# First pair's in, out and query projections as three products of float32r parts, in a transformer-like trunk on one Trainium2 core

## Chip, cores, metric

One core of one Trainium2 chip runs the whole program. The metric is the time of one execution on the device, in microseconds (us), as the median of several runs. The engines named below: TensorE (PE in the rows; its weight loads PEld), VectorE (DVE), ScalarE (ACT), GpSimd (POOL) and SyncE (SP), which issues most transfers.

## What is computed

One layer on 1024 tokens of width 1024: a normalised input goes through an in-projection to three token mixers (a gated depthwise convolution of width 31, a short gated convolution of width 3, a gated block mixing), then through an out-projection; a query projection and product keys choose 16 of 16384 single-neuron experts for each of 8 heads; the chosen experts' rows are applied; an input embedding gate and a final norm end it.

```python
a = rmsnorm(h, g_mix[i])
z = a @ w_in[i]
za, zb, zc = z[..., :768], z[..., 768:1536], z[..., 1536:]
...
h = h + jnp.concatenate([ya, yb, yc], axis=-1) @ w_out[i]
...
q = (nf @ w_q).reshape(t, PEER_HEADS, D_KEY)
s1 = jnp.einsum("thd,hkd->thk", q1, sub_keys[:, 0])
v1, i1 = lax.top_k(s1, TOPK)
...
act = jax.nn.gelu(jnp.einsum("td,tkd->tk", xb, expert_u[ib])) * gb
out = jnp.einsum("tk,tkd->td", act, expert_v[ib])
```

## The kernel before

The 1024 tokens are eight tiles of 128 (the partition width). The front works on pairs of tiles, (0,1), (2,3), (4,5), (6,7); T = 256 columns a pair. `mix_in` (L139) loads and normalises the pair's rows, transposes them into `aT` (L148, 8 chunks of 128 inputs x 256 tokens) and makes 15 chunks of 128 outputs in `zchunks` (L152: one 512 KB weight tile `w1` and 8 float32 matmuls a chunk, into the PSUM tile `z`), and three more with `aT` as the stationary side (L201 to L208, the tile `vn`). The convolution (L177 to L180) is 30 x 3 VectorE steps `cacc = ya * ch + cacc`, all three tiles in SBUF. Statistics of `vn` follow (L209 to L223; the power of -1/2, `rv`, L220, is GpSimd's), then a mixing product (L232), a group norm of the convolution (L239 to L252), and the 8 chunks of `yT`.

`mix_out` (L255) multiplies `yT` with `w_out` (L267, 256 float32 records a pair), adds the residual (L269), normalises and transposes into `nT`. `choose` (L283) makes the queries, 16 chunks of 8 matmuls (L299), the key scores (L306), 16 best of each by VectorE (`top16`, L327) and `select` (L335), whose last step writes the gather index `idx` (L392).

Four of the tiles (`DENSE`, 1 to 4) go through all experts in a later stage, three (`GATHER`, 5 to 7) gather rows, and the `MIXED` tile 0 does its first half by gathers in the front: `u_step` (L524) issues 128 row gathers on GpSimd's queue (L536) with a VectorE dot product each (L538), and `gate_table` (L394) builds tables with VectorE, GpSimd (`oh2`, L421), ScalarE and TensorE. The dense stage starts when these are done, after some 1090 us; there and at the end of the program the products are already made of float32r parts: `hi` by a ScalarE cast, `lo = full - hi` by a GpSimd subtraction (L468 and L470), and three products hi*hi, hi*lo, lo*hi (L481 to L483).

A framework's scheduler sets the order on each engine when the program is built, from the program's order and its own estimates; each engine then runs its list strictly in that order and waits on semaphores. Small pools hold what rotates: `gathF` has three tiles `g` and one `hrow` for the gathers; `wstream` two each of `w1`, `wo`, `w3` for weights; `wbp` two tiles `st` for the tables.

## Time and profile before

| | us |
|---|---|
| median of 3 runs (2859.8 to 2860.92) | 2860.1 |
| the profiled execution | 2848.63 |
| its span, first to last instruction | 2846.6 |
| TensorE busy | 2607.7 (92%) |
| VectorE busy | 2163.0 (76%) |
| GpSimd busy | 1951.6 (69%) |
| ScalarE busy | 1007.2 (35%) |

The busy share is an average over stages with different limits; the dense stage, from some 1090 us on, holds most of TensorE's time. The change lies in the first 350 us, so the rows further down are read by stretch. Matmuls are pipelined: a single record's length says less than the time of a run of them divided by their number. A float32 matmul stands in the trace as two records.

### The profile page before, as it was taken

To read this page: it belongs to the slowest core of one execution; us is meant where nothing else is said; L and a number is where in the kernel's file an instruction comes from. 1 tells how busy PE (TensorE), PEld (TensorE's weight loads), DVE (VectorE), ACT (ScalarE), POOL (GpSimd) and SP (SyncE) were. 2 spreads that over 40 slices of the span, in tenths; PEclk is the share of its full clock that TensorE was granted. 3 is DMA by queue.
4 is the path that set the end of the run, shared out by engine and by line. 5 is a ranking of instruction groups with operands and counts; after the bars stand their busy time and mean duration, and the time that the engine had idled before them with its cause. 6 is when DMAs were issued, how large, how long until landed. Compare 5 with 4: busy or idle time off the path is not lost.

```text
span 2846.6 us, 37627 instructions
## 1 busy us (share of the span) xinstructions
PE 2607.7 (92%) x12671; PEld 2197.8 (77%) x12671; DVE 2163.0 (76%) x4738; ACT 1007.2 (35%) x1930; POOL 1951.6 (69%) x1740
## 2 busy tenths in 40 slices
PE   7999989798768568999999999999999999999988
PEld 6888878787767556888787888878788787888777
DVE  5566998899977886777777777776777777777776
ACT  3324237345655534232322223222232322222352
POOL 0000067368776787887888878887887878888783
PEclk9999999899778779999999999999999999999999
DMA  6354577787757559999999999999999999999885
GB/s 209 121 194 146 190 269 275 283 299 268 236 210 268 207 211 337 329 338 334 330 346 326 336 343 344 337 332 335 335 335 325 332 351 323 341 337 328 312 290 174
DMA packets 299697, 820.92 MB, mean 288 GB/s; under 512 B 26096, under 2 KB 117616, under 8 KB 296944
## 3 DMA queue, kind: packets, MB, share of 16 engines
q0 software_dynamic: 129024, 469.82, 45.9%
q1 hardware_dynamic: 170480, 348.70, 36.0%
q8 instruction: 100, 1.64, 0.2%
q14 instruction: 93, 0.76, 0.1%
HBM read 764.93 MB, written 53.48 MB: 288 GB/s over the span
## 4 chain that ended last, share of the span: by engine, by line
PE 43%; DVE 18%; DMA 18%; POOL 11%; issue 8%; ACT 1%; SPq 0%; POOLq 0%; DVEq 0%; ACTq 0%
DMA g<-expert_u,idx 8%; DMA g<-expert_v,idx 7%; PE mm L504 5%; PE mm L505 5%; PE mm L506 5%; PE z L481 5%; PE z L482 5%; PE z L483 5%; DVE g L538 4%; POOL g L536 3%; PE z L158 3%; PE mm L612 3%; POOL oh L421 3%; POOL vl L477 3%; PE mm L299 2%
## 5 line engine op out<-in xcount | busy, mean ns | idle before, releaser
L536 POOL DMA_INDIRECT g<-expert_u,idx x512 | 509.5, 995 | 340.1 <-DVE g L538 137.1
L568 DVE SCALAR_TENSOR_TENSOR accP<-g,act,accP 128x1024 f32<-128x1024 f32 x384 | 493.6, 1285 | 205.3 <-DMA g<-expert_v,idx 199.9
L538 DVE SCALAR_TENSOR_TENSOR g<-g,nP 128x1024 f32<-128x1024 f32 x352 | 423.2, 1215 | 168.9 <-DMA g<-expert_u,idx 167.7
L566 POOL DMA_INDIRECT g<-expert_v,idx x384 | 367.2, 956 | 143.4 <-DVE accP L568 62.0
L504 PE MATMUL mm<-vh,ah 128*128 128x512 f32 x1024 | 399.8, 392 | 16.1 <-DVE accA L508 8.8
L481 PE MATMUL z<-nh,uh 128*128 128x512 f32 x1024 | 401.5, 392 | 8.1 <-DVE al L490 5.9
L482 PE MATMUL z<-nl,uh 128*128 128x512 f32 x1024 | 400.2, 391 | 1.6 <-DVE nl L446 1.5
L483 PE MATMUL z<-nh,ul 128*128 128x512 f32 x1024 | 399.8, 390 | 0.0
L505 PE MATMUL mm<-vl,ah 128*128 128x512 f32 x1024 | 398.7, 390 | 0.0
L506 PE MATMUL mm<-vh,al 128*128 128x512 f32 x1024 | 396.4, 390 | 0.0
L421 POOL TENSOR_SCALAR oh<-iota,eT,gT 128x128 f32<-128x128 f32 x320 | 325.2, 1024 | 43.7 <-PE gt L430 39.0
L430 PE MATMUL gt<-oh,oh 128*128 128x128 f32 x1280 | 228.0, 327 | 131.6 <-DVE oh L415 69.7
L468 ACT CAST uh<-u 128x1024 fp32r<-128x1024 f32 x128 | 134.7, 1052 | 566.9 <-PE z L482 449.5
L477 POOL TENSOR_TENSOR vl<-v,vh 128x512 fp32r<-128x512 f32 x256 | 327.5, 1300 | 2.6
L430 PEld LDWEIGHTS gt<-oh,oh 128*128 128x128 f32 x1280 | 199.5, 229 | 160.7 <-POOL oh L421 92.1
L470 POOL TENSOR_TENSOR ul<-u,uh 128x1024 fp32r<-128x1024 f32 x128 | 308.7, 2412 | 3.9 <-ACT uh L468 1.9
L475 ACT CAST vh<-v 128x512 fp32r<-128x512 f32 x256 | 153.7, 621 | 319.1 <-DMA v<-expert_v 266.6
L538 DVE SCALAR_TENSOR_TENSOR g<-g,hrow 128x1024 f32<-128x1024 f32 x160 | 196.4, 1230 | 74.5 <-DMA g<-expert_u,idx 74.3
L299 PE MATMUL mm<-nT,w 128*128 128x256 f32 x1024 | 243.1, 387 | 0.0
L504 PEld LDWEIGHTS mm<-vh,ah 128*128 128x128 f32 x1024 | 193.0, 189 | 59.3 <-DVE accA L508 11.8
L508 DVE TENSOR_TENSOR accA<-mm,accA 128x512 f32<-128x512 f32 x320 | 218.1, 685 | 26.2 <-PE mm L506 25.6
L481 PEld LDWEIGHTS z<-nh,uh 128*128 128x128 f32 x1024 | 193.6, 189 | 53.0 <-DVE al L490 10.6
(367 smaller groups left out, 4593.6 us busy)
## 6 DMA issues: line engine op xcount, KB each, us to landing
u<-expert_uT SPq DMA_DIRECT2D x128, 512.0 KB, 6.1
v<-expert_v SPq DMA_DIRECT2D x128, 512.0 KB, 5.0
Wd<-st SPq DMA_DIRECT2D x20, 2048.0 KB, 8.9
w<-w_q SPq DMA_DIRECT2D x64, 512.0 KB, 4.5
w<-Wd SPq DMA_DIRECT2D x128, 256.0 KB, 10.2
w<-w_inF SPq DMA_DIRECT2D x60, 512.0 KB, 4.1
wo<-w_out SPq DMA_DIRECT2D x32, 512.0 KB, 3.4
g<-expert_u,idx POOLq DMA_INDIRECT x512, 6.2
```

Of the source, the lines that this page charges most:

```text
L421: nc.gpsimd.tensor_scalar(oh2[:, k], iota, k2, gk, op0=OP.is_equal, op1=OP.mult)
L430: nc.tensor.matmul(pw[:, :, k], oh2[:, k], oh1[:, k], start=True, stop=True)
L477: nc.gpsimd.tensor_tensor(vl, v[:, s * 512:s * 512 + 512], vh.bitcast(F32), op=OP.subtract)
L481: nc.tensor.matmul(ph, uh[:, c], nh[:, c], start=c == 0, stop=False)
L482: nc.tensor.matmul(ph, uh[:, c], nl[:, c], start=False, stop=False)
L483: nc.tensor.matmul(ph, ul[:, c], nh[:, c], start=False, stop=c == 7)
L504: nc.tensor.matmul(po, ah[:, c], vh, start=i == 0, stop=False)
L505: nc.tensor.matmul(po, ah[:, c], vl, start=False, stop=False)
L506: nc.tensor.matmul(po, al[:, c], vh, start=False, stop=i == NG - 1)
L536: nc.gpsimd.indirect_dma_start(out=ug, out_offset=None, in_=expert_u, in_offset=bass.IndirectOffsetOnAxis(ap=idx[:, k:k + 1], axis=0))
L538: nc.vector.scalar_tensor_tensor(ug, ug, 1.0, ns[t, front], op0=OP.mult, op1=OP.mult, accum_out=dots[:, k - b * KB:k - b * KB + 1])
L568: nc.vector.scalar_tensor_tensor(acc, vg, act[:, k:k + 1], acc, op0=OP.mult, op1=OP.add)
```

## The change

For the first pair (`t0` = 0) alone, the three projections are computed from float32r parts. `in_halves` splits the activations into `hi` (ScalarE) and `lo` (GpSimd), 16 pieces of 128x128 each for `aT` and `nT`, 8 of 128x256 for `yT`; they lie in the three `g` tiles and `hrow` of the gather pool. `weight_halves` splits one or two weight chunks of 128x1024 into a tile `st` of the pool that the gate tables use later. `add_up` adds 24 products for each output in place of 8. Two weight chunks are taken at a time; the raw weights alternate between two pairs of buffers. The three narrow chunks of the in-projection are computed 256 columns wide (the odd one with a repeated operand), and the out-projection two chunks of 128 columns at a time.

```diff
@@ -74,6 +74,10 @@
     nTd = dram.tile([P, 8, NA * P], F32, name="nTd")
     TG = 32
     Wd = {t: dram.tile([P, P // TG, P, TG], F32, name=f"Wd{t}") for t in TABLE}
+
+
+    SPLIT_IN, SPLIT_OUT, SPLIT_Q = (0,), (0,), (0,)
+    CHUNKS = (3, 4, 5, 6, 7, 0, 1, 2)
 
     fctx = ExitStack()
     work = fctx.enter_context(tc.tile_pool(name="work", bufs=2))
@@ -134,7 +138,34 @@
                 for c in range(4):
                     nc.scalar.activation(dst[:, c0 + c], pt[:, c], AF.Copy, scale=g[:, c0 + c:c0 + c + 1])
 
-    picks, keys, weights = {}, {}, {}
+    def in_halves(full, parts, order=range(8)):
+
+        T = full.shape[2]
+        lie = [gath.tile([P, 4, T], F32R, name=n, bufs=b) for n, b in (("g", FG), ("g", FG), ("g", FG), ("hrow", 1))]
+        hi = {c: lie[2 * (i // 4)][:, i % 4] for i, c in enumerate(order)}
+        lo = {c: lie[2 * (i // 4) + 1][:, i % 4] for i, c in enumerate(order)}
+        for p in parts:
+            for c in order:
+                nc.scalar.copy(hi[c][:, p], full[:, c, p])
+                nc.gpsimd.tensor_tensor(lo[c][:, p], full[:, c, p], hi[c][:, p].bitcast(F32), op=OP.subtract)
+        return [(hi[c], lo[c]) for c in range(8)]
+
+    def weight_halves(*raws):
+
+        w = wbp.tile([P, 2, 2, 8, P], F32R, name="st")
+        for i, raw in enumerate(raws):
+            nc.scalar.copy(w[:, 0, i], raw)
+            nc.gpsimd.tensor_tensor(w[:, 1, i], raw, w[:, 0, i].bitcast(F32), op=OP.subtract)
+        return w
+
+    def add_up(out, a, b):
+
+        order = CHUNKS
+        steps = [(a[c][x_], b[c][y_]) for x_, y_ in ((0, 0), (0, 1), (1, 0)) for c in order]
+        for i, (a_, b_) in enumerate(steps):
+            nc.tensor.matmul(out, a_, b_, start=i == 0, stop=i == len(steps) - 1)
+
+    picks, keys, weights, turn = {}, {}, {}, [0]
 
     def mix_in(t0, nt):
 
@@ -147,10 +178,22 @@
             nc.scalar.activation(a, a, AF.Copy, scale=r)
             transpose_rows(aT[:, :, t * P:(t + 1) * P], a, g_mix, tag="z")
 
+        if t0 in SPLIT_IN:
+            aH = in_halves(aT, [slice(t * P, (t + 1) * P) for t in range(nt)])
         yT = group.tile([P, 8, T], F32, name="yT")
 
         def zchunks(*js):
             pz = psum.tile([P, 2, T], F32, name="z")
+            if t0 in SPLIT_IN:
+                raws = []
+                turn[0] += 1
+                for j in js:
+                    raws.append(wstream.tile([P, 8, P], F32, name=("w1", "w3")[turn[0] % 2], bufs=2))
+                    nc.sync.dma_start(raws[-1], w_inF[j])
+                w = weight_halves(*raws)
+                for i in range(len(js)):
+                    add_up(pz[:, i], [(w[:, 0, i, c], w[:, 1, i, c]) for c in range(8)], aH)
+                return [pz[:, i] for i in range(len(js))]
             for i, j in enumerate(js):
                 w = wstream.tile([P, 8, P], F32, name="w1", bufs=2)
                 nc.sync.dma_start(w, w_inF[j])
@@ -198,7 +241,21 @@
 
 
         vn = group.tile([P, nt, 384], F32, name="vn")
-        for s in range(3):
+        for ss in ((0, 1), (2,)) if t0 in SPLIT_IN else ():
+            raws = []
+            turn[0] += 1
+            for s in ss:
+                raws.append(wstream.tile([P, 8, P], F32, name=("w1", "w3")[turn[0] % 2], bufs=2))
+                nc.sync.dma_start(raws[-1], w_inV[s])
+            w, n = weight_halves(*raws), len(ss)
+
+            wh, wl = [w[:, x_] if n == 2 else w[:, x_, 0:1].to_broadcast([P, 2, 8, P]) for x_ in range(2)]
+            for t in range(nt):
+                pv = psum.tile([P, 2, P], F32, name="z")
+                p = slice(t * P, (t + 1) * P)
+                add_up(pv, [(h_[:, p], l_[:, p]) for h_, l_ in aH], [(wh[:, :, c], wl[:, :, c]) for c in range(8)])
+                nc.scalar.copy(vn[:, t, ss[0] * P:(ss[0] + n) * P].rearrange("p (a c) -> p a c", a=n), pv[:, 0:n])
+        for s in () if t0 in SPLIT_IN else range(3):
             wv = wstream.tile([P, 8, P], F32, name="w1", bufs=2)
             nc.sync.dma_start(wv, w_inV[s])
             for t in range(nt):
@@ -258,7 +315,23 @@
         nT = group.tile([P, 8, T], F32, name="nT")
         hs = rowp.tile([P, nt, D], F32, name="h", bufs=1)
         nc.sync.dma_start(hs, x[t0 * P:(t0 + nt) * P].rearrange("(t p) d -> p t d", p=P))
-        for s in range(8):
+        if t0 in SPLIT_OUT:
+            yH = in_halves(yT, [slice(0, T)], CHUNKS)
+        for s in range(0, 8, 2) if t0 in SPLIT_OUT else ():
+            raws = []
+            for i in range(2):
+                raws.append(wstream.tile([P, 8, P], F32, name=("wo", "w3")[s // 2 % 2], bufs=2))
+                nc.sync.dma_start(raws[-1], w_out[s + i])
+            w = weight_halves(*raws)
+            po = psum.tile([P, nt, 2 * P], F32, name="mm")
+            for t in range(nt):
+                p = slice(t * P, (t + 1) * P)
+                add_up(po[:, t].rearrange("p (a c) -> p a c", a=2), [(h_[:, p], l_[:, p]) for h_, l_ in yH],
+                       [(w[:, 0, :, c], w[:, 1, :, c]) for c in range(8)])
+            h = hs[:, :, s * P:s * P + 2 * P]
+            nc.vector.tensor_add(h, po, h)
+            fill()
+        for s in () if t0 in SPLIT_OUT else range(8):
             w = wstream.tile([P, 8, P], F32, name="wo", bufs=2)
             nc.sync.dma_start(w, w_out[s])
             po = psum.tile([P, nt, P], F32, name="mm")
@@ -278,6 +351,8 @@
         if own:
             a0 = DENSE.index(t0 + own[0]) * P
             nc.sync.dma_start(nTd[:, :, a0:a0 + len(own) * P], nT[:, :, own[0] * P:(own[-1] + 1) * P])
+        if t0 in SPLIT_Q:
+            return in_halves(nT, [slice(t * P, (t + 1) * P) for t in range(nt)])
         return nT
 
     def choose(t0, nt, nT):
@@ -292,7 +367,15 @@
             pq = psum.tile([P, 2, T], F32, name="mm")
             sk = wstream.tile([P, 2, P], F32, name="sk", bufs=2)
             nc.sync.dma_start(sk, skT[:, 2 * h:2 * h + 2])
-            for side in range(2):
+            if t0 in SPLIT_Q:
+                raws = []
+                for side in range(2):
+                    raws.append(wstream.tile([P, 8, P], F32, name=("w3", "wo")[h % 2], bufs=2))
+                    nc.sync.dma_start(raws[-1], w_q[2 * h + side])
+                w = weight_halves(*raws)
+                for side in range(2):
+                    add_up(pq[:, side], [(w[:, 0, side, c], w[:, 1, side, c]) for c in range(8)], nT)
+            for side in () if t0 in SPLIT_Q else range(2):
                 w = wstream.tile([P, 8, P], F32, name="w3", bufs=2)
                 nc.sync.dma_start(w, w_q[2 * h + side])
                 for c in range(8):

```

Three places show how the order on the engines moves. First GpSimd, from its first `r` on (before: the norm factors `r`, `rB` and `rv`, and nothing else up to the gathers):

```order
L122 TENSOR_TENSOR r_150<-ss_147,half 128x1
L122 TENSOR_TENSOR r_177<-ss_174,half 128x1
L122 TENSOR_TENSOR r_862<-ss_859,half 128x1
L122 TENSOR_TENSOR r_889<-ss_886,half 128x1
L220 TENSOR_TENSOR rv<-st,half 128x6 x2
L122 TENSOR_TENSOR r_2748<-ss_2745,half 128x1
L122 TENSOR_TENSOR r_2775<-ss_2772,half 128x1
L122 TENSOR_TENSOR rB<-ss_818,half 128x1
L122 TENSOR_TENSOR rB<-ss_837,half 128x1
L220 TENSOR_TENSOR rv<-st,half 128x6 x2
```

and now (`st<-w` is the low part of a weight chunk, `g` and `hrow` low parts of `aT`):

```order
L126 TENSOR_TENSOR r_150<-ss_147,half 128x1
L126 TENSOR_TENSOR r_177<-ss_174,half 128x1
L158 TENSOR_TENSOR st<-w_236,st 128x1024
L158 TENSOR_TENSOR st<-w_238,st 128x1024
L158 TENSOR_TENSOR st<-w_300,st 128x1024
L150 TENSOR_TENSOR g<-aT,g 128x128 x2
L158 TENSOR_TENSOR st<-w_302,st 128x1024
L150 TENSOR_TENSOR g<-aT,g 128x128 x2
L150 TENSOR_TENSOR hrow<-aT,g 128x128 x4
L150 TENSOR_TENSOR g<-aT,g 128x128 x4
L150 TENSOR_TENSOR hrow<-aT,g 128x128 x4
L126 TENSOR_TENSOR r_1361<-ss_1358,half 128x1
L126 TENSOR_TENSOR r_1388<-ss_1385,half 128x1
```

Subtractions stand between the norm factors; 18 of weights and 16 of `aT` come ahead of the first `rv`.

Second VectorE, at the end of the first pair's convolution. Before (the statistics of `vn` start behind the 90th convolution step):

```order
L179 SCALAR_TENSOR_TENSOR cacc<-ya,ch,cacc 128x256 x2
L197 TENSOR_TENSOR yT<-z,bacc 128x256
L179 SCALAR_TENSOR_TENSOR cacc<-ya,ch,cacc 128x256 x15
L212 TENSOR_REDUCE st<-vn 128x6
L213 TENSOR_SCALAR st<-st 128x6
L214 TENSOR_TENSOR vn<-vn,st 128x384
L212 TENSOR_REDUCE st<-vn 128x6
L217 TENSOR_REDUCE st<-vsq 128x6
```

and now:

```order
L222 SCALAR_TENSOR_TENSOR cacc<-ya,ch,cacc 128x256 x3
L240 TENSOR_TENSOR yT<-z,bacc 128x256
L222 SCALAR_TENSOR_TENSOR cacc<-ya,ch,cacc 128x256 x21
L269 TENSOR_REDUCE st<-vn 128x6
L222 SCALAR_TENSOR_TENSOR cacc<-ya,ch,cacc 128x256 x2
L270 TENSOR_SCALAR st<-st 128x6
L222 SCALAR_TENSOR_TENSOR cacc<-ya,ch,cacc 128x256 x2
L271 TENSOR_TENSOR vn<-vn,st 128x384
L222 SCALAR_TENSOR_TENSOR cacc<-ya,ch,cacc 128x256
L269 TENSOR_REDUCE st<-vn 128x6
L222 SCALAR_TENSOR_TENSOR cacc<-ya,ch,cacc 128x256 x2
L274 TENSOR_REDUCE st<-vsq 128x6
```

The statistics now stand among the last convolution steps, still behind nearly all of them: L275, which `rv` waits for, comes behind 87.

Third TensorE, from the mixing product of the first pair to the first products of the second. Before:

```order
L232 MATMUL z<-wsT,vn 64x128 x4
L242 MATMUL z<-cacc,blk 128x256 x2
L247 MATMUL z<-csq,blk 128x256
L242 MATMUL z<-cacc,blk 128x256
L247 MATMUL z<-csq,blk 128x256
L130 MATMUL z<-ident,a 128x128 x8
L267 MATMUL mm<-wo,yT 128x128 x4
L130 MATMUL z<-ident,a 128x128 x4
L247 MATMUL z<-csq,blk 128x256
L130 MATMUL z<-ident,a 128x128 x4
L158 MATMUL z<-aT,w_912 128x256 x8
L158 MATMUL z<-aT,w_922 128x256 x4
```

and now (`mm<-st,g` are out-projection products of the first pair):

```order
L289 MATMUL z<-wsT,vn 64x128 x4
L166 MATMUL mm<-st,g 128x256 x4
L299 MATMUL z<-cacc,blk 128x256 x2
L166 MATMUL mm<-st,g 128x256 x6
L304 MATMUL z<-csq,blk 128x256
L299 MATMUL z<-cacc,blk 128x256
L304 MATMUL z<-csq,blk 128x256
L134 MATMUL z<-ident,a 128x128 x12
L166 MATMUL mm<-st,g 128x256 x2
L304 MATMUL z<-csq,blk 128x256
L166 MATMUL mm<-st,g 128x256 x2
L134 MATMUL z<-ident,a 128x128 x4
```

The second pair's transposes and its first chunk (`L201`, before `L158`) stand behind the group norm of the first pair in both.

## Rows read from the trace of the kernel before

**Rows 1.** busy us (count) by stretch: PE, PEld, DVE, ACT, POOL, clock, DMA

```profile
31.00:82.00 51.00, 48.48 (x266) 42.40 (x266) 46.15 (x113) 8.50 (x26) 2.41 (x2) 1.00 0.42 136
82.00:105.00 23.00, 17.03 (x86) 11.92 (x85) 9.64 (x18) 12.66 (x29) 1.35 (x2) 0.85 0.27 89
105.00:279.00 174.00, 173.04 (x1010) 155.29 (x1011) 109.19 (x385) 54.18 (x109) 6.43 (x7) 0.99 0.49 163
279.00:348.00 69.00, 66.39 (x444) 61.58 (x444) 68.68 (x305) 19.55 (x35) 1.63 (x2) 1.00 0.51 167
350.00:1090.00 740.00, 582.34 (x3347) 517.41 (x3346) 635.55 (x2178) 380.24 (x885) 522.36 (x501) 0.87 0.72 255
```

**Rows 2.** chain by line at 100–270, 270–350 and 350–720 us

```profile
by line: PE z L158 31.6%; PE mm L299 24.6%; PE mm L267 16.3%; PE z L207 6.3%; PE mm L306 3.8%; DMA h1d<-h 3.0%; DMA a<-x 1.9%; PE mm L130 1.1%; PE z L232 1.1%; PE z L130 1.0%; DVE csq L250 0.9%; DVE h L275 0.8%; ACT L249 0.8%; ACT junk L118
...
by line: DVE cacc L179 35.1%; DMA g<-expert_u,idx 9.5%; DVE s L332 6.9%; DVE pos L334 4.3%; DVE pos L330 4.3%; DVE oh L375 3.8%; DVE oh L377 3.3%; DVE h L269 3.3%; DVE oh L374 3.1%; DVE h L275 3.0%; DVE vals L333 2.9%; DVE vals L329 2.9%; D
...
by line: DMA g<-expert_u,idx 27.7%; DVE g L538 16.5%; issue 8.4%; POOL oh L421 7.8%; DVE cacc L179 6.9%; DVE oh L415 5.8%; POOL g L536 3.7%; DVE s L332 2.9%; DVE ti L330 2.7%; DVE tv L329 2.3%; DVE tv L333 1.5%; DVE csq L250 1.3%; DVE oh L3
```

**Rows 3.** L179 from 31 to 82 us: ns min/median/max, first to last start

```profile
L179 DVE SCALAR_TENSOR_TENSOR cacc<-ya,ch,cacc x90: 473/480/485, 31.0 to 73.0; 128x256 f32<-128x256 f32 x90
```

**Rows 4.** chain in order of time: start us, us, matmul records

```profile
118.46 3.46 PE z L158 x16
121.92 7.14 PE mm L267 x64
...
2758.92 12.29 PE mm L612 x54
```

**Rows 5.** single lines (ns min/median/max), and one group of the page

```profile
L208 ACT COPY vn<-z x24: 245/265/270, 67.2 to 625.8; 128x128 f32<-128x128 f32 x24
...
L605 POOL TENSOR_TENSOR pTl<-pT,pTh x8: 732/736/757, 2726.8 to 2809.1; 128x256 fp32r<-128x256 f32 x8
...
L470 POOL TENSOR_TENSOR ul<-u,uh x128: 2355/2412/2607, 967.3 to 2649.9; 128x1024 fp32r<-128x1024 f32 x128
...
L468 ACT CAST uh<-u 128x1024 fp32r<-128x1024 f32 x128 | 134.7, 1052 | 566.9 <-PE z L482 449.5
```

**Rows 6.** timeline (start us, us) of two meetings, and their lines

```profile
973.71 2.61 POOL L470 TENSOR_TENSOR ul<-u,uh 128x1024 fp32r<-128x1024 f32 x1
974.24 2.15 DVE L344 TENSOR_TENSOR cand<-tv 128x64 f32<-128x64 f32 x1
...
L344 DVE TENSOR_TENSOR cand<-tv x8: 198/205/2154, 291.5 to 974.2; 128x64 f32<-128x64 f32 x8
...
2735.20 1.31 POOL L682 TENSOR_TENSOR wpe11l<-wr,wpe11h 128x512 fp32r<-128x512 f32 x1
...
2735.86 1.21 DVE L622 TENSOR_TENSOR accA<-accA,sg 128x512 f32<-128x512 f32 x1
...
L622 DVE TENSOR_TENSOR accA<-accA,sg x10: 680/682/1206, 2735.9 to 2798.1; 128x512 f32<-128x512 f32 x10
```

**Rows 7.** timeline of a meeting the other way, and the line L421 (min/median/max)

```profile
971.86 1.22 DVE L538 SCALAR_TENSOR_TENSOR g<-g,hrow 128x1024 f32<-128x1024 f32 x1
971.96 1.78 POOL L421 TENSOR_SCALAR oh<-iota,eT,gT 128x128 f32<-128x128 f32 x1
...
L421 POOL TENSOR_SCALAR oh<-iota,eT,gT x320: 780/792/2957, 385.2 to 1081.4; 128x128 f32<-128x128 f32 x160
```

**Rows 8.** timeline of the start: aT complete, first products

```profile
18.93 2.17 ACT L135 ACTIVATE aT<-z,ch 128x128 f32<-128x128 f32 x8 [0.18 <-PE z L130]
20.12 7.17 PE L158 MATMUL z<-aT,w 128*128 128x256 f32 x32 [0.24 <-ACT aT L135]
```

**Rows 9.** timeline of GpSimd: the first gather

```profile
348.10 1.37 POOL L536 DMA_INDIRECT g<-expert_u,idx  x1 [16.84 <-DVE idx L392]
```

## The prediction

> **What bounds the kernel now.** I read the busy time by stretch first [rows 1]. From 105 to 279 us TensorE is busy 173.0 of 174 us and VectorE only 109.2: the products of the first two pairs of token tiles set the pace. From 279 to 348 us it is the reverse, VectorE 68.7 of 69 us. From 350 to 1090 us no engine is full (VectorE 635.6, TensorE 582.3, GpSimd 522.4 of 740). The chain that ended last says the same in other words [rows 2]: TensorE's projections up to 270 us, then VectorE's convolution and top-16 steps, then the row gathers with VectorE's dot products. The hinge is the start of the gathers: the first one is issued at 348.10 us, after GpSimd had waited 16.84 us for VectorE's `idx` of the mixed tile [rows 9]. Behind that point the order of the gathers and gate-table steps is almost the same in both kernels (by the 128th gather VectorE has 98 `oh1` steps behind it before and 96 after), and nothing of the change is left. So I forecast by how much the `idx` of the mixed tile moves, and let the end move with it. The change lies wholly before it, in five stretches: the start (to 31 us), the convolution of the first pair (31 to 82), its tail (82 to 105), the products of two pairs interleaved (105 to 279) and VectorE's backlog (279 to 348).
>
> **TensorE's products.** A float32 chunk of 256 columns takes 3.46 us for 16 records; one of 128 columns 7.14/64 = 0.112 us a record [rows 4]. The first pair's work was 15 chunks of the in-projection (51.9 us), 96 narrow records for its last three chunks (10.7), 256 for the out-projection (28.6) and 16 query chunks (55.4): 146.6 us. In its place stand 360 + 96 + 192 + 384 = 1032 float32r products of 256 columns. The trace has float32r only at 512 columns, 12.29/54 = 0.2276 us each [rows 4]. Half of that, 0.114, is the low end; the narrow float32 record of 0.112 plus the 0.011 by which 0.2276 exceeds a wide float32 record (3.46/16 = 0.216) gives 0.123; no gain from the smaller width, 0.2276, is a rival below. I take 0.114, since the 512-column row is the only one with these operands: 117.4 us, 29 less (20 less at 0.123). Of this the out and query parts, 576 products, are 65.5 against 84.0 us: 18.5 us less in the stretch where TensorE is the bound (13.2 at 0.123). The rest falls into a stretch that VectorE will bound.
>
> **GpSimd and ScalarE.** Each of 42 weight chunks now costs a ScalarE cast, 1.05 us, and a GpSimd subtraction, 2.41 us; 128x256 takes 0.736 us, so 2.18 ns a column and 0.18 us fixed, and 128x128 some 0.46 [rows 5]. GpSimd gets 42 x 2.41 + 32 x 0.46 + 8 x 0.74 = 122 us, in a stretch where it did next to nothing (2.4, 1.4, 6.4 us in the first three of rows 1). ScalarE gets 44 + 11 = 55 us and was busy under a third. Alone, GpSimd keeps pace: 2.41 us a chunk against 24 x 0.114 = 2.7 on TensorE. The bytes loaded are the same, with four raw buffers in place of two. The shared ring `g`, `hrow` is held until the first pair's last query product; its next user, the mixed tile's row, isn't needed before 348 us, so this costs nothing unless the queries end later than that.
>
> **The start, +6 us.** The scaled `aT` was complete at 18.93 + 2.17 = 21.1 us and the first product ran at 20.12 [rows 8]. Now four casts of weights and 16 casts of pieces (0.27 each, rows 5) stand in ScalarE's order, and on GpSimd four weight subtractions and 16 pieces, 9.6 + 7.3 = 17 us from about 16.5 us, when the first cast ends. The first pair of chunks needs the last low piece, at about 34 us, so the convolution starts at some 37 us in place of 31.0 [rows 3].
>
> **VectorE and GpSimd stop each other.** This is the largest term. A VectorE addition of 64 columns with both inputs in SBUF takes 0.205 us; the one at 974.24, begun while GpSimd subtracted from 973.71 to 976.32, took 2.15 and ended 0.08 us behind it. At the end of the program an addition of two SBUF tiles took 1.206 in place of 0.682 under a subtraction that ended at 2736.51 [rows 6]. The other way, a GpSimd step of 0.79 us took 1.78 us when VectorE's two-input dot product had begun 0.1 us earlier, and up to 2.96 [rows 7]. Where one VectorE input is in PSUM nothing is seen: 128 subtractions of the dense stage have a median of 2.412 [rows 5] beside VectorE sums into `accP`. The convolution step reads `ya` and `cacc`, both in SBUF, 90 times a pair at 0.48 us [rows 3]. So in the first pair the two queues add up. Some five of the 18 weight subtractions are over by 37 us; 13 remain ahead of `rv`, which waits for the statistics that VectorE's order puts behind 87 convolution steps. VectorE's own work of that stretch is 46.2 us [rows 1]; 13 holds of 2.23 us (2.41 less the fixed part) make 29.0; 4.6 us of VectorE's steps there (reductions and those with a PSUM input) can run under a hold. 37 + 46.2 + 29.0 - 4.6 = 107.6 us in place of 82: **+25.6**, start included. Bounds: +22 if more of VectorE's steps slip under, +33 with a quarter of a us lost at each hand-over and full 2.41 us holds. TensorE, once done with its chunks, stands idle there: the order gives it the second pair's products only behind the first pair's statistics, as before. The tail keeps its shape (VectorE 9.6 of 23 us busy): -0.7 us for its one chunk at 24 x 0.114.
>
> The Trainium skill, page SBUF — State Buffer, section Who interferes with whom, states such a rule: a VectorE instruction with two SBUF inputs contends with a GpSimd instruction that reads SBUF, and whoever starts first keeps the shared pair of ports for the whole instruction. By it the 13 holds would be 31.4 us, not 29.0, and the sum 2.4 us higher; the rows agree to within the fixed 0.18 us of an instruction.
>
> **From the tail to the gathers.** TensorE's solid run starts 25 us later and is 18.5 us shorter: its end goes from 279 to some 285. For this VectorE has to keep up: 109.2 us of work, and 20 more weight subtractions plus 16 pieces, some 49 us of holds, of which I let half block it, against 155.5 us: 134 us, it does. In the backlog VectorE has 12 steps fewer ahead of `idx` (241 convolution steps in place of 251, 10 of `bacc` in place of 12), -5 us. They come later, where VectorE is busy 86%: +2, between 0 and 5.
>
> **Sum:** +25.6 - 0.7 - 18.5 - 5 + 2 = +3.4 us. The profiled execution took 2848.63 us (span 2846.6); the median of the runs shown is 2860.1, 11.5 more, and I carry that over: 2863.5, say **2864**. With each term at its ends this case spans 2858 to 2879. A difference of 0.2%, 5.7 us, is about what a measurement of this kernel tells from no change; the forecast lies just inside it.
>
> **Rivals.** *The collision costs little:* GpSimd's subtractions fall where VectorE waits anyway (it idles 65 us of 174 from 105 on). The trace shows too few pairs of long steps to know how often they meet. Then only the start's 6 us remains, and the sum is 6 - 0.7 - 18.5 - 5 + 2 = -16: 2844, with 2836 to 2852 around it. Against it stands that from 31 to 82 us VectorE is 90% busy, nearly all with two-input steps. *Slower: VectorE becomes the bound from 105 on too.* Its convolution of the second pair meets the out and query subtractions. If all 49 us of holds block it and it still waits 20 us for TensorE's heads, the stretch takes 109 + 49 + 20 = 178 us in place of 155.5, and the sum is 22 higher: 2886; with the holds at two thirds 2870. It decides as soon as blocking and unavoidable waiting together pass 46 us. *The products do not get cheaper with width:* 1032 x 0.2276 = 235 us in place of 147, 88 more on TensorE, most of it on the path: 2930 or more. A second form of the same: weights and products don't overlap at 256 columns.
>
> **How the numbers follow.** Forecast 0.42 (faster 0.03, same 0.25, slower 0.14); collision cheap 0.28 (faster 0.26, same 0.02); VectorE bound 0.22 (slower 0.20, same 0.02); no gain from width 0.05; the rest, an order of queues that turns out otherwise in the long middle, 0.03 (faster 0.02, slower 0.01). Faster 0.31, same 0.29, slower 0.40. The range takes in the bounds of the forecast, most of the cheap case and of the slower one, and leaves out the last two: 2840 to 2884.
>
> **What would show it.** In the changed trace: products of 256 columns at 0.114 to 0.123 us; convolution steps from 37 us on of up to 2.5 us each, not 0.48, wherever a subtraction of 2.41 stands beside them; `rv` of the first pair near 107 us, TensorE idle for some 30 us ahead of it; the first gather within 10 us of 348 plus the sum. If the convolution steps keep 0.48 us the collision is wrong and the first gather should come near 330; if the second pair's steps are long as well and the gather comes near 370, VectorE is the bound. If the gather moves and the end doesn't, it is the middle that I have wrong.

## The result, and the profile after

The changed kernel took 2894.8 us (median of 4 runs, 2891.3 to 2910.8), the kernel before 2860.5 in the same job: a ratio of 1.0129 [1.0099, 1.0158], 34.3 us slower. The forecast was 2864, with 2840 to 2884 around it. The profiled execution took 2891.3 us (span 2889.3).

A ledger of five marks shows where the time went; it is read from one profiled execution of each kernel. The marks are the second `rv` of the first pair, the first wide in-product of the second pair (TensorE's solid run starts), the copy of the eighth query head (it ends), the first gather, and the first product of the value stage.

| us | second `rv` | to solid run | solid run | to first gather | first gather at | to value stage |
|---|---|---|---|---|---|---|
| before | 81.2 | 24.0 | 173.7 | 69.2 | 348.1 | 760.4 |
| after | 111.5 | 30.7 | 166.1 | 69.4 | 377.7 | 765.2 |
| difference | +30.3 | +6.7 | −7.6 | +0.2 | +29.6 | +4.8 |
| forecast | +25.6 | −0.7 | −18.5 | −5 | +1.4 | +2 |

Most of the loss, 29.6 of the 34.3 us, is there at the first gather. Two extracts of the changed kernel's trace answer to [rows 1] and [rows 3]. The first is busy time by stretch, columns as in [rows 1]; the second the convolution step L222 in the first pair and in the second (ns min/median/max).

```profile
37.00:110.00 73.00, 52.74 (x386) 51.62 (x384) 68.66 (x107) 21.28 (x41) 40.85 (x15) 0.88 0.31 101
110.00:135.00 25.00, 13.12 (x76) 10.25 (x76) 16.26 (x23) 11.53 (x23) 15.16 (x11) 0.72 0.24 79
142.20:308.20 166.00, 154.74 (x1055) 144.09 (x1056) 114.88 (x369) 72.56 (x141) 64.50 (x44) 0.98 0.48 159
308.20:377.70 69.50, 66.74 (x444) 61.56 (x443) 68.90 (x307) 19.09 (x34) 1.55 (x3) 1.00 0.50 161
```

```profile
L222 DVE SCALAR_TENSOR_TENSOR cacc<-ya,ch,cacc x90: 468/473/2620, 41.5 to 112.6; 128x256 f32<-128x256 f32 x90
...
L222 DVE SCALAR_TENSOR_TENSOR cacc<-ya,ch,cacc x90: 471/485/2544, 163.2 to 223.2; 128x256 f32<-128x256 f32 x90
```

The median step is as before, the longest five times as long: 13 steps of the first pair took over 1 us, 24.7 us more than they would have. I call such a step held, and the time that it loses a hold. VectorE counts as busy for 68.66 of 73 us, while TensorE idles 20. The timeline shows a meeting (start us, us; `x` counts instructions in a row): from 59.51 us GpSimd makes two weight subtractions. The first takes 5.33 us in place of 2.42, with seven convolution steps in a row beside its first 3 us; then it is VectorE's turn to wait, and it needs 4.79 us for two steps.

```profile
57.39 5.22 DVE L222 SCALAR_TENSOR_TENSOR cacc<-ya,ch,cacc 128x256 f32<-128x256 f32 x13
62.53 0.42 DVE L232 TENSOR_TENSOR mb<-z,sg 128x256 f32<-128x256 f32 x1
62.87 4.79 DVE L222 SCALAR_TENSOR_TENSOR cacc<-ya,ch,cacc 128x256 f32<-128x256 f32 x2
...
59.51 7.87 POOL L158 TENSOR_TENSOR st<-w,st 128x1024 fp32r<-128x1024 f32 x2 [6.86 <-ACT st L157]
```

The solid run lost 10 us by a way that the prediction did not name. The timeline of GpSimd, VectorE, SP's queue (SPq) and TensorE from 169 to 195 us, and SP's longest wait on line 346, read as one chain:

```profile
169.46 4.94 POOL L158 TENSOR_TENSOR st<-w,st 128x1024 fp32r<-128x1024 f32 x2 [5.33 <-ACT st L157]
175.15 4.84 POOL L158 TENSOR_TENSOR st<-wo,st 128x1024 fp32r<-128x1024 f32 x2 [0.75 <-ACT st L157]
...
170.14 12.21 DVE L222 SCALAR_TENSOR_TENSOR cacc<-ya,ch,cacc 128x256 f32<-128x256 f32 x9
182.27 0.68 DVE L332 TENSOR_TENSOR h<-mm,h 128x512 f32<-128x512 f32 x1
...
182.98 0.81 SPq L346 DMA_DIRECT2D h1d<-h  x2
183.88 0.74 SPq L199 DMA_DIRECT2D w<-w_inF  x1
...
SPq L346 <- DVE h L332: 8.1, 1, 8.1
...
189.63 5.16 PE L201 MATMUL z<-aT,w 128*128 128x256 f32 x16 [8.77 <-DMA w<-w_inF]
```

Four subtractions stretch nine convolution steps to 12.21 us. Behind them in VectorE's order stands the addition to `h`; SP's queue waits 8.1 us for it to store `h`; behind the store stands the load of the second pair's next weights; and TensorE waits 8.77 us for that load. VectorE is busy only 114.88 of the run's 166 us: it is not the bound there, it is late.

### The profile page after: what moved, and what is told of

Same layout as the page of the kernel before. It is cut to its first block, busy times and chain, and to the rows that moved or that the text cites. A ratio compares the mean times of both kernels' runs of the same rounds, so it can differ in the third digit from the quotient of the medians.

```text
span 2889.3 us, 38221 instructions
## 1 busy us (share of the span) xinstructions
PE 2602.2 (90%) x12855; PEld 2203.3 (76%) x12855; DVE 2203.7 (76%) x4734; ACT 1054.5 (36%) x2009; POOL 2094.1 (72%) x1822
## 4 chain that ended last, share of the span: by engine, by line
PE 38%; DVE 21%; DMA 19%; POOL 12%; issue 8%; ACT 2%; SPq 0%; POOLq 0%; DVEq 0%; ACTq 0%
DMA g<-expert_u,idx 8%; DMA g<-expert_v,idx 8%; PE mm L587 5%; PE mm L589 5%; PE mm L588 5%; PE z L564 4%; PE z L565 4%; DVE cacc L222 4%; PE z L566 4%; DVE g L621 4%; PE mm L695 3%; POOL g L619 3%; POOL oh L504 3%; POOL vl L560 3%; PE z L201 2%
## 5 line engine op out<-in xcount | busy, mean ns | idle before, releaser
L504 POOL TENSOR_SCALAR oh<-iota,eT,gT 128x128 f32<-128x128 f32 x320 | 336.7, 1059 | 56.4 <-PE gt L513 52.5
L565 PEld LDWEIGHTS z<-nl,uh 128*128 128x128 f32 x1024 | 193.6, 189 | 43.7 <-DVE nl L529 3.8
```

Of the source, the lines that this page charges most:

```text
L504: nc.gpsimd.tensor_scalar(oh2[:, k], iota, k2, gk, op0=OP.is_equal, op1=OP.mult)
L565: nc.tensor.matmul(ph, uh[:, c], nl[:, c], start=False, stop=False)
```

## Experiments: the collision

All ratios are to the kernel before, in the same job. "From parts" means three float32r products in place of one in float32. The first diffs are against the changed kernel.

**no_sub.** The subtractions are left out, and the products read the high part in place of the low one: the same number of products, other values.

```diff
-                nc.gpsimd.tensor_tensor(lo[c][:, p], full[:, c, p], hi[c][:, p].bitcast(F32), op=OP.subtract)
-        return [(hi[c], lo[c]) for c in range(8)]
+        return [(hi[c], hi[c]) for c in range(8)]
...
-            nc.gpsimd.tensor_tensor(w[:, 1, i], raw, w[:, 0, i].bitcast(F32), op=OP.subtract)
...
-                    add_up(pz[:, i], [(w[:, 0, i, c], w[:, 1, i, c]) for c in range(8)], aH)
+                    add_up(pz[:, i], [(w[:, 0, i, c], w[:, 0, i, c]) for c in range(8)], aH)
```

> All subtractions on GpSimd are left out; each product that read a low part reads the high part instead, so casts, loads and TensorE's 1032 products stay. Theory (VectorE and GpSimd stop each other while GpSimd subtracts): the 13 convolution steps of 2.3 to 2.6 us in the first pair go back to 0.48 us, the first rv comes at 80 to 88 us in place of 108.7, the first gather at 335 to 345, the time at 2840 to 2860. Rival (the casts in ScalarE's order, which wait behind steps of VectorE, and the start): rv stays above 100 us, the time at 2885 or more.

2847.5 us, 0.9961 [0.9941, 0.9981]. The first `rv` is at 80.0 us and no convolution step is over 0.49. The solid run takes 154.2 us (forecast 155.5), and the first gather comes at 326.8, sooner than I expected and 21 us earlier than before. Yet the time is only 12 us less.

**psum_acc.** In the first two pairs the convolution adds into PSUM, so that each step has one input in SBUF; ScalarE copies the sums back. All subtractions stay.

```diff
-            acc = work.tile([P, T], F32, name="cacc", bufs=3)
+            if t0 in (0, 2):
+                acc = psum.tile([P, 4, P], F32, name="gt", bufs=3)[:, 0:2].rearrange("p a c -> p (a c)")
+            else:
+                acc = work.tile([P, T], F32, name="cacc", bufs=3)
...
+            if t0 in (0, 2):
+                acc = work.tile([P, T], F32, name="cacc", bufs=3)
+                nc.scalar.copy(acc, accs[j])
```

> The changed kernel with the convolution's running sum of the first two pairs in PSUM instead of SBUF (in the three banks that the gate tables use later), copied back once by ScalarE. All subtractions stay. Theory (only two SBUF inputs meet GpSimd): no convolution step over 0.7 us, rv at 82 to 92 us, first gather at 340 to 352, time 2848 to 2868. Rival (ScalarE's order and the start): nothing moves by more than 5 us, 2890 to 2900. Rival (memory traffic of GpSimd in general slows VectorE): steps still up to 2.5 us, 2890 to 2900.

2861.9 us, 1.001 [0.9987, 1.0032]: 33 of the 34 us are gone. The line of its steps, and a meeting like the one above:

```profile
L225 DVE SCALAR_TENSOR_TENSOR gt<-ya,ch,gt x180: 472/484/491, 40.3 to 190.5; 128x256 f32<-128x256 f32 x180
...
59.81 1.26 DVE L225 SCALAR_TENSOR_TENSOR gt<-ya,ch,gt 128x256 f32<-128x256 f32 x3
60.98 0.41 DVE L243 TENSOR_TENSOR yT<-z,bacc 128x256 f32<-128x256 f32 x1
61.32 1.65 DVE L225 SCALAR_TENSOR_TENSOR gt<-ya,ch,gt 128x256 f32<-128x256 f32 x4
...
59.56 2.58 POOL L158 TENSOR_TENSOR st<-w,st 128x1024 fp32r<-128x1024 f32 x1
...
67.14 1.39 DVE L240 SCALAR_TENSOR_TENSOR bacc<-mb,ch,bacc 128x256 f32<-128x256 f32 x1
...
63.24 7.52 POOL L158 TENSOR_TENSOR st<-w,st 128x1024 fp32r<-128x1024 f32 x3 [1.09 <-ACT st L157]
```

Under the subtraction at 59.56 us VectorE makes five steps of 0.48 us; held steps of the changed kernel took up to 2.62 us each. The step `bacc` (L240) still has both inputs in SBUF, and in the same trace it is still held: 1.39 us at 67.14, in place of 0.47. What the PSUM sum does by itself, in the kernel before, is the run before_psum further down.

**psum_first, psum_second.** The same edit with `t0 == 0` or `t0 == 2` alone.

> The change with the convolution sum of the first pair alone in PSUM; the second pair's stays in SBUF. If the first pair's 13 long steps carry most of the loss, the first rv comes near 85 us, the second convolution still has 3 or more steps over 1 us, and the time is 2860 to 2874 us, 20 to 30 below the change. If the loss sits in the second pair's collisions, 2878 to 2890.

> The change with the convolution sum of the second pair alone in PSUM. If the first pair carries most of the loss: first rv near 108 us, 13 long steps, 2880 to 2894 us, 2 to 12 below the change. If the second pair does: 2862 to 2874.

psum_first 2871.1 us, 1.0033 [1.0007, 1.0058], first `rv` 85.8; psum_second 2886.2, 1.0089 [1.006, 1.0118], first `rv` 107.4. The loss divides: 24 us to the first pair, 9 to the second, together psum_acc's 33. In psum_first (L225 by form; SP's and TensorE's waits) the second pair's long steps and the chain behind them are still there:

```profile
L225 DVE SCALAR_TENSOR_TENSOR gt<-ya,ch,gt x90: 473/479/491, 41.0 to 89.7; 128x256 f32<-128x256 f32 x90
L225 DVE SCALAR_TENSOR_TENSOR cacc<-ya,ch,cacc x90: 471/485/2493, 139.1 to 200.6; 128x256 f32<-128x256 f32 x90
...
SPq L352 <- DVE h L338: 8.1, 1, 8.1
...
PE z L201 <- DMA w<-w_inF: 9.4, 2, 9.1
```

In psum_acc TensorE waits 2.3 us for `w_inF` in the same stretch, and the solid run is 158.3 us against 166.2. psum_second agrees: SP's queue waits 0.3 us for `h` and TensorE 4.1 us for `w_inF`, and the run takes 161.3 us.

**in_only, outq_only.** The projections apart: `SPLIT_OUT, SPLIT_Q = (), ()`, and `SPLIT_IN = ()`.

> Only the in-projection of the first pair from parts; out and query in float32 as before. Theory: the whole of the first pair's delay stays (rv near 108 us, TensorE's solid run 30 to 37 us late) and TensorE gets nothing back later, so slower than the full change: 2895 to 2910. Rival (the out and query parts are what costs, through VectorE's second convolution): 2865 to 2880.

> Only the out and query projections of the first pair from parts. Theory: rv of the first pair as before, near 81 us; TensorE's stretch from 105 us on is 14 to 18 us shorter, minus what the second convolution loses to 20 subtractions (8 to 15 us): 2848 to 2864. Rival (out and query parts cost as well): 2870 to 2885.

in_only 2884.2 us, 1.0096 [1.006, 1.0132]; outq_only 2867.2, 1.0032 [1.001, 1.0054]. Both fell between the theories: the in-projection alone carries the first pair's 13 long steps (first `rv` 108.6), the other two put 7 on the second pair's convolution, and the two effects, +25 and +8 us, leave little for an interaction.

**sub_quarter.** Each weight subtraction cut into four of 128x256.

```diff
-            nc.gpsimd.tensor_tensor(w[:, 1, i], raw, w[:, 0, i].bitcast(F32), op=OP.subtract)
+            for k in range(0, 8, 2):
+                nc.gpsimd.tensor_tensor(w[:, 1, i, k:k + 2], raw[:, k:k + 2], w[:, 0, i, k:k + 2].bitcast(F32), op=OP.subtract)
```

> The change with each weight subtraction cut into four of 128x256 (0.74 us each by rows 5, 2.9 us a chunk in place of 2.41). If the time for which GpSimd holds the ports is what counts, the number of long convolution steps grows about fourfold, each near 0.7 to 1.1 us, the first rv stays at 105 to 113 us and the time at 2888 to 2905. If a long single hold is the trouble (VectorE slips in between short ones for nothing), rv comes at 90 to 98 us and the time at 2868 to 2880.

2871.7 us, 1.0037 [1.0015, 1.006], and the first `rv` at 108.4. The `rv` is the first theory's, the time the second's. The lines of the steps and of the subtractions, and a meeting:

```profile
L223 DVE SCALAR_TENSOR_TENSOR cacc<-ya,ch,cacc x180: 466/485/1040, 43.2 to 215.4; 128x256 f32<-128x256 f32 x180
...
L159 POOL TENSOR_TENSOR st<-w,st x120: 720/901/3439, 16.5 to 280.5; 128x256 fp32r<-128x256 f32 x120
...
64.01 4.12 DVE L223 SCALAR_TENSOR_TENSOR cacc<-ya,ch,cacc 128x256 f32<-128x256 f32 x5
...
62.17 8.31 POOL L159 TENSOR_TENSOR st<-w,st 128x256 fp32r<-128x256 f32 x8 [3.45 <-ACT st L157]
```

The engines now take turns at short holds: five steps in 4.12 us, none over 1.04. The long steps cost 17.0 us there in place of 24.7, but the convolution also started 1.7 us later. In the profiles the first gather is 6 us and the end 12 us earlier than in the changed kernel, half of the 23 us between the medians. The profiled execution is the slowest of seven here and the fastest of four in the changed kernel, so part of the rest is the choice of executions; the remainder stays open.

## Experiments: what sets the pace

no_sub left a question: why did 21 us at the gather bring only 12? Over the kernels so far VectorE's busy time up to the value stage and the time of that stage moved together (before 886 us and 1108, no_sub 878 and 1101, psum_acc 894 and 1114, the change 928 and 1143). I took for a theory (a) that VectorE sets the time wherever its work lies, against (b), TensorE sets it from 105 to 279 us, as the prediction had it.

**halves_only.** All parts are made, and the products use the raw float32 values.

```diff
-                    add_up(pz[:, i], [(w[:, 0, i, c], w[:, 1, i, c]) for c in range(8)], aH)
+                    for c in range(8):
+                        nc.tensor.matmul(pz[:, i], raws[i][:, c], aT[:, c], start=c == 0, stop=c == 7)
```

> The change with every cast, subtraction and buffer of it, but its products are those of the kernel before: float32 on the raw weights and activations; the parts are made and not read. Two readings stand against each other. (a) VectorE sets the time up to the first product of the value stage: there the trace before has VectorE busy 886.1 us and idle 222.4, the change 927.6 and 215.2, the variant without subtractions 878.0 and 222.7, so TensorE's saving is worth no more than some 7 us. Then this kernel, with the collisions and without the saving, ends at 2890 to 2905 us. (b) The saving of 18.5 to 29 us on TensorE is real and hidden under the collisions' cost: then it ends at 2912 to 2925. Both expect the first pair's first rv near 105 to 112 us and 13 or so convolution steps of 2.3 to 2.6 us.

2908.5 us, 1.0169 [1.0139, 1.0198], between the two. The collisions are there (steps of up to 2.58 us, first `rv` 110.9). The products from parts are worth 14 us: the solid run takes 184.4 us in place of 166.1.

**before_load.** The kernel before, with 36 VectorE steps more in the second pair's convolution, which multiply by zero.

```diff
+            for j in range(3):
+                if t0 == 2 and k < 13:
+                    nc.vector.scalar_tensor_tensor(accs[j], yas[j][:, k:k + T], zero[:, 0:1], accs[j],
+                                                   op0=OP.mult, op1=OP.add)
```

> The kernel before with 36 more VectorE steps in the convolution of the second pair: the first twelve taps are followed by a step of the same form that multiplies by zero, 36 x 0.45 = 16 us of VectorE, in a stretch that the prediction called TensorE's (105 to 279 us) and in which VectorE idled 65 us. (a) If VectorE's busy time sets the time up to the value stage wherever it is spent, 2870 to 2884 us. (b) If TensorE is the bound there, 2855 to 2866.

2861.1 us, 1.0011 [0.9992, 1.0031]: (a) falls. Its stretch from 105 to 279 us, beside [rows 1]:

```profile
105.00:279.00 174.00, 171.34 (x1002) 153.25 (x1003) 119.34 (x408) 56.09 (x111) 6.48 (x8) 0.99 0.48 160
```

TensorE is full, VectorE takes on 10 us more, and the solid run grows by 0.7 us. 13 us more VectorE work cost nothing there, whereas 11.5 us of holds (VectorE busy 248.2 us up to the first gather in psum_first, 236.8 in psum_acc) cost 9: in before_load SP's queue never waits for `h`.

**before_taps, before_taps2, after_taps2.** 13 of the 31 taps become TensorE products with diagonal matrices; the sums of the first two pairs are in PSUM in all three. The taps are moved in the first pair of the kernel before, in its first two pairs, and in the first two pairs of the changed kernel.

```diff
+                    for k in range(KT):
+                        dg = work.tile([P, P], F32, name="s2", bufs=4)
+                        nc.scalar.activation(dg, ident, AF.Copy, scale=ch[:, j * 31 + k:j * 31 + k + 1])
+                        nc.tensor.matmul(acc, dg, yas[j][:, k:k + T], start=k == 0, stop=k == KT - 1)
```

> The kernel before with the convolution sums of the first two pairs in PSUM, and the first 13 of the 31 taps of the first pair done by TensorE as products with diagonal matrices that ScalarE builds: 36 VectorE steps less (16 us), 39 products of 0.216 us more on TensorE (8 us) in a stretch where it is idle half the time. Both readings give 2832 to 2846 us, 2850 less some 4 to 18; if nothing is gained over the PSUM variant of the kernel before, neither holds.

> As the variant with 13 taps of the first pair on TensorE, with the same in the second pair: there VectorE has 16 us less again and TensorE 8 us more. (a) VectorE sets the time: 8 to 16 us less than with the first pair alone, 2820 to 2836. (b) TensorE is the bound from 105 to 279 us: 2 to 8 us more than with the first pair alone, 2840 to 2852.

> The change with the convolution sums of the first two pairs in PSUM and 13 of their 31 taps on TensorE: the collision is gone, VectorE has 32 us less than the kernel before and TensorE some 20 us less net. (a) VectorE sets the time: about that of the same edit on the kernel before, 2822 to 2842 us. (b) If TensorE's saving reaches the end, 15 us or more below it, 2805 to 2820.

2877.4 us, 1.0058 [1.0034, 1.0082]; 2897.7, 1.0126 [1.009, 1.0162]; 2889.8, 1.0093 [1.0058, 1.0128]. All three expectations missed, by an error of mine: a float32 product of 256 columns is two records of 0.216 us (3.46 us is 16 records and 8 products [rows 4]), so the 39 products of a pair cost 16.8 us and not 8; and TensorE was not idle half the time there, as I had written, but busy 48.5 of 51 us [rows 1]. before_taps shows it, in the first pair's stretch:

```profile
31.00:94.00 63.00, 63.00 (x338) 56.58 (x337) 33.77 (x72) 20.47 (x61) 0.19 (x1) 1.00 0.32 109
```

VectorE has 12 us less, TensorE is full, and the first `rv` comes 15 us later. It fits (b) once more, and the chain of the kernel before says the same: from 40.40 to 77 us it holds TensorE's products and the load of `w_inV`, and no convolution step. TensorE, with the loads of its weights, sets the pace there too.

**before_psum, outq_psum, q_psum.** The PSUM sum of psum_acc in the kernel before; with out and query from parts; with the query alone.

> The kernel before, with only the convolution sum of the first two pairs in PSUM and its copy back by ScalarE: what that edit does by itself. Expected within 0.3% of the kernel before, 2852 to 2868 us, convolution steps at 0.48 to 0.50 us. If it were faster by 10 us or more, a part of what the PSUM variant of the change won back would not be the collision's.

> Out and query projections from parts, the in-projection in float32, and the convolution sum of the first two pairs in PSUM (copied back by ScalarE), so that no subtraction meets a VectorE step with two SBUF inputs there. If VectorE's busy time sets the time up to the value stage, it is near the kernel before: 2852 to 2868 us, though TensorE's stretch ends some 18 us earlier. If TensorE's saving reaches the end, 2838 to 2848.

> Only the query projection from parts, the convolution sums of the first two pairs in PSUM: TensorE saves 16 x 3.46 - 384 x 0.12 = 9 us in the stretch that it sets, and the start and the first pair are those of the kernel before. If a gain at the last query head is passed on to the end, 2836 to 2850 us; if it is given back behind the first gather, where VectorE then has more steps left, 2850 to 2864.

| | time, us | ratio | solid run | first gather | to value stage |
|---|---|---|---|---|---|
| before_psum | 2850.2 | 0.996 [0.9942, 0.9979] | 178.2 | 352.7 | 746.2 |
| outq_psum | 2861.6 | 1.0 [0.9983, 1.0017] | 158.1 | 336.2 | 790.5 |
| q_psum | 2846.6 | 0.9944 [0.9916, 0.9972] | 167.8 | 345.4 | 756.5 |

before_psum missed its expectation: it is 12 us faster than the kernel before, and I had written that from 10 us on a part of what psum_acc won back would not be the collision's. At the marks this does not show: the PSUM sum alone has the first `rv` at 78.2 us in place of 78.8 and the first gather 4.6 us later, whereas in the changed kernel it brought the `rv` forward by 23.6 us and the gather by 31.9. At the end it may: of the 33 us that psum_acc won back, 21 to 33 are the collision's, and with the PSUM sum in both kernels the change still costs 12 us.

Against before_psum, TensorE's saving shows in the solid run, 20 and 10 us, and in the first gather, 16.5 and 7 us. It does not show in the time: outq_psum is 11 us slower, and q_psum 4 us faster, which is inside the intervals. The trace of no_sub gives a reason, from its first gather to the 128th and on to the value stage (columns as in [rows 1]):

```profile
326.80:859.90 533.10, 453.37 (x2748) 411.10 (x2747) 481.86 (x1644) 279.08 (x659) 357.18 (x330) 0.92 0.75 263
859.90:1100.70 240.80, 155.02 (x749) 131.76 (x747) 185.41 (x603) 117.51 (x254) 191.29 (x181) 0.75 0.68 245
```

VectorE is busy 667.3 us there, against 650.1 in the kernel before: 47 steps that stood ahead of the first gather stand behind it (786 ahead of it, and 833 before). Apart from its work VectorE waits there mostly for gathered rows, and about as long as before (71.3 us in 37 waits, before 75.3 in 36): 17.2 us more work, and the stretch is 13.6 us longer. Of the 21 us by which the first gather came early, TensorE's shorter run gave 19.5 and a shorter backlog 7.7, less 5.8 at the start and the tail; VectorE's work that had fitted beside the longer run was left for later. In outq_psum the work is 8.5 us more than in the kernel before (658.6) and the waits for rows 13.1 more (88.4 in 41), together 21.6 of the 30.1 us by which the stretch is longer; why the rows are waited for longer stays open, and so does why the PSUM sum alone shortens the stretch by 14 us. Each of these traces is one execution, and the executions of the kernel before lie between 2849 and 2884 us in one job, so a difference of this size behind the gather is read with care. q_psum is the fastest kernel that computes everything, 14 us below the kernel before, and inside the range in which the gain is passed on, but its interval overlaps before_psum's: that the query from parts adds to it is not shown.

## Why the prediction was wrong, step by step

**What held.** The products: 48 of the seventh head's queries stand in the chain of waits as one entry, 0.120 us each, inside the 0.114 to 0.123 of the forecast.

```profile
290.62 5.75 PE mm L166 x48
```

The subtractions' price (2.42 us in the median, as in [rows 5]). The holds ahead of the first `rv`: 14 subtractions ran behind 37 us and each held one step, 13 of the convolution (eleven of them 2.3 to 2.6 us long, the others 1.2 and 2.1) and one of the statistics. And the `rv` itself, forecast 107.6 us, measured 108.7. psum_acc and no_sub show that this meeting is the cause of the delay. The first two steps of the tail show it too, on multiplications of 0.57 us each (timeline of VectorE and GpSimd):

```profile
113.09 2.69 DVE L278 TENSOR_TENSOR vn<-vn,rv 128x384 f32<-128x384 f32 x1
115.81 2.58 DVE L279 TENSOR_TENSOR vn<-vn,lnc 128x384 f32<-128x384 f32 x1
...
113.02 4.95 POOL L158 TENSOR_TENSOR st<-wo,st 128x1024 fp32r<-128x1024 f32 x2
```

The Trainium skill, page SBUF — State Buffer, section Who interferes with whom, states that a VectorE instruction with at most one SBUF input does not contend with GpSimd, unless it runs in one of VectorE's 2-port modes; psum_acc agrees, with steps of at most 0.491 us beside subtractions. One step with a single SBUF input was held all the same: `st` (L270, 128x6) took 2.35 us at 102.36, where its like at 107.99 took 0.16. Whether it ran in such a mode no run shows.

**Step 1, the convolution: +25.6 forecast, +29.9 measured at the first `rv`, +30.3 at the second.** The time of `rv` was right within 1.1 us; it was the other end that I took wrongly, "82 us", which is the boundary of a stretch in [rows 1]. The kernel before has it at 78.8 (timeline of GpSimd):

```profile
78.84 1.58 POOL L220 TENSOR_TENSOR rv<-st,half 128x6 f32<-128x6 f32 x1 [48.75 <-DVE st L218]
```

The start was +10.5 us and not +6 (41.5 against 31.0). The low parts were ready at 32.7 us, sooner than the 34 of the forecast; behind them I had 3 us for the products and nothing for ScalarE, where the chain has

```profile
31.10 7.51 PE z L166 x44
...
39.02 1.88 ACT st L157 x2
```

From the first step to `rv` the forecast had 70.6 us (46.2 of VectorE's own work, 29.0 of holds, 4.6 run under them), and it was 67.2: no_sub needs 41.2 without holds, the 13 held convolution steps cost 24.7, the held `st` 2.2. So a start 4.5 us later than forecast and a stretch 3.4 us shorter cancel, and that `rv` was right within 1.1 us is in part luck.

**Step 2, the tail: −0.7 forecast, +6.7 measured.** I held that it "keeps its shape", since VectorE was busy only 9.6 of 23 us there. Three things in the chain stand against it. The out weights' subtractions fall on `vn` (above, 4.2 us more in two steps). TensorE, which had been busy 52.74 of the 73 us ahead, has a granted clock of 0.72 on average, against 0.85 before: it is 0.50 (1.2 GHz) from 113 to 124 us, where the same place before has 1.00, and the products of the first entry below follow each other at 0.21 us in place of 0.12. And casts of parts stand in ScalarE's order ahead of the group norm:

```profile
120.25 3.79 PE z L166 x16
124.07 1.14 ACT g L149 x4
...
125.66 1.89 ACT st L157 x2
```

no_sub, without any subtraction, has +4.0 there, psum_acc +6.1, in_only, whose out-projection is the float32 one, +2.6. How much of the 6.7 is due to each of the three no run told apart.

**Step 3, the solid run: −18.5 forecast, −7.6 measured.** The size of TensorE's saving was right: without collisions the run is 154 to 158 us, against 155.5. This is the largest miss. What failed is the sentence that VectorE keeps up because 134 us of work fit into 155.5. The sum fits, and the order doesn't: a step that is late at one place holds up SP's queue, and TensorE waits 10.1 us for two loads (1.5 in no_sub, 2.3 in psum_acc). The rival "VectorE becomes the bound" had the place and, with 162 to 178 us for this run, about the size; its time of 2870 to 2886 still fell short of 2894.8, for it kept the other terms. Its mechanism, a full VectorE, is refuted by 114.88 busy of 166 us. The sign that I had set for it, long steps in the second pair and a gather near 370 us, came true all the same: it doesn't tell a full VectorE from a late one. I had named no queue behind the holds.

**Step 4, the backlog: −5 forecast, +0.2 measured.** From the eighth head to the first gather it is 69.2 to 69.5 us in the kernel before, the change, psum_acc, psum_first, psum_second, before_psum, before_load, sub_quarter and q_psum. VectorE is full there (68.90 of 69.5 us; 68.68 of 69 in [rows 1]) with the same work, 307 steps against 305: the 12 steps that I counted out are missing earlier (819 steps up to the gather against 833), not in this stretch.

**Step 5, the end moves with the first gather.** For the change it held roughly: +29.6 at the gather, +34.3 at the value stage, +34.3 in the median, but +42.7 between the two profiled executions. As a rule it is wrong for gains, as no_sub and outq_psum show, and for losses too: in_only has +35.8 at the gather and +25 in the median, sub_quarter +23.6 and +10. That it served here is luck.

Steps 1 to 4 miss by 4.7, 7.4, 10.9 and 5.2 us, together the 28 us between the forecast of +1.4 and the measured +29.6 at the gather. All four were taken too favourably, and the range did not let their errors add.

## What to carry over

Before giving GpSimd a long elementwise step, look for VectorE steps with two SBUF inputs in the same stretch, and put one operand of them into PSUM: here that won back 33 of 34 us, 12 of which the same edit also gave in the kernel before. An engine with idle time in a stretch can still hold up the stretch: follow what stands behind a delayed step, in its own engine's order and in the DMA queue that stores its result. A saving ahead of a backlog is only worth what the next stretch doesn't take back, so ask which steps will then stand behind the mark.

## What was not expected of the hardware

Where subtractions follow each other, about one VectorE step passes for each: two in 4.79 us under long ones, five in 4.12 us under quarters. But the hand-over is not always one for one, and GpSimd pays as well. The subtraction at 59.51 us took 5.33 us in place of 2.42: seven convolution steps of 0.48 us passed in a row, and it ended 2.31 us, about its own length, after VectorE had come to `mb` (L232, 62.53 us), which has one input in PSUM. In halves_only one took 8.36 us. The subtraction at 82.70, on the other hand, ended at 85.26 and so waited for hardly one step. What decides between the two no run told apart. The quarters of 0.72 us had a median of 0.901 in the line above.

```profile
L158 POOL TENSOR_TENSOR st<-w,st x30: 2333/2422/5330, 16.4 to 284.0; 128x1024 fp32r<-128x1024 f32 x30
```
